# A hybrid decoder trunk on one core: which output block is kept in a gate's tile, where short rows of logits stand, and how the last square of a norm is added

## The chip, the cores and the metric

The kernel runs on one core of a Trainium2 chip. Its time is the device time of one execution in microseconds (us). The core's engines run their own instruction streams and wait for each other through semaphores: TensorE (PE) multiplies matrices into PSUM, VectorE (DVE) and ScalarE (ACT) work on tiles, GpSimd (POOL) and SyncE (SP) here mostly issue transfers (DMA). An engine takes its instructions strictly in order, so an instruction that waits holds all that stand behind it.

## The reference

Two layers over 1024 positions of width 1024, each with a residual and an RMS norm ahead, and a last norm behind. All is float32.

```python
def reference(x, norm_g, final_g, lru_..., fox_...):
    for i in range(DEPTH):                       # DEPTH = 2
        h = rms_norm(x, norm_g[i])
        if i % N_MIXERS == 0:
            x = x + lru_mixer(h, ...)
        else:
            x = x + fox_mixer(h, ...)
    return rms_norm(x, final_g)

def rms_norm(x, g):
    y = x * rsqrt(mean(x * x, axis=-1) + EPS)
    return y * g

# lru_mixer: u = h @ w_in; a causal convolution of 4 taps; two gates, block-diagonal (12 blocks of 128);
#            a linear recurrence along the positions; times silu(gate); @ w_out
# fox_mixer: 16 heads of 64; logits = q @ k.T / 8 + (cum_q - cum_k), causal; softmax; @ v; times silu(gate); @ w_out
```

## The kernel before

**Form of the data.** Activations lie transposed: 128 channels of a block on the partitions, the positions along the free axis, in two halves of 512 (`HALF`; c or h is 0 or 1). A float32 product is made of three matmuls: each operand is split into a high part and a remainder (`to_hi`, `to_lo`: hh and hl, wh and wl, yhh and yhl), and hh·wh, hh·wl and hl·wh are summed in PSUM. A product of a 128x512 block with k input blocks is thus 3k matmuls of 128x512.

**Order.** A scheduler places the instructions of each engine by a timeline of its own; the code gives priorities, and `issue_after` ties an instruction behind another. So a small edit can move instructions elsewhere.

**Layer 0** (to about 432 us). `square_x` squares the eight input blocks of a half on ScalarE and adds seven of them into one tile on VectorE; the eighth square stays in its own tile. `norm_row` sums both tiles over the channels with two products with a matrix of ones (`rsrow`), accumulated, then a square root (ScalarE) and a reciprocal (VectorE) give the row `rs` by which products are scaled. Then twelve channel blocks run through input product (`ups`, `gps`), convolution (`us`, `xc`, its split `xch`, `xcl`), gates (`gate`), recurrence and output. `softplus` computes small constants of all blocks from one 128x12 parameter (`sp_e`, `sp_d`, `sp_q`), on VectorE.

**Boundary** (about 432 to 475 us). The last output product is added to the residual, which is written to memory as `x1d`, split and squared again (`squares`). Here too the last square of a half is left in its own tile (`wait=db == KT - 1`), and `inv_rms` sums over channels with matmuls of one column per 128 positions (`sscol`), as many as there are tiles.

**Layer 1** (about 475 to 1057 us): sixteen heads. For a head hd and a half c, `maxima` makes four rows of logits (`S`; row i has 128(i+1) columns: rows 0 to 3 for c = 0, rows 4 to 7 for c = 1), VectorE masks them and takes the maximum, ScalarE the exponential (`p`), the two split it into half-precision parts (`pp`), and SyncE issues a DMA that transposes them (`pT`). `weigh` multiplies pT with the values into `O`. `run(order, ...)` (L855) lays these out on TensorE: in `ORDER` and `LAST`, "1" is a row of logits, "0" a step of weighing and "." a step of fill, which is six matmuls of some other product. A head has two runs: the first weighs its half 0 and makes its rows 4 to 7, the second weighs its half 1 and makes rows 0 to 3 of the next head. `ORDER` holds for heads 0 to 11, `LAST` for the rest. Fill is the projections of the next heads (`gps`, `vps` among the value heads 3, 7 and 11, where new values are made), and from head 12 on the blocks (db, c) of the output projection, in the order (0,0), (1,0), (0,1), (1,1), (2,0), (2,1), (3,0), (3,1), (4,0) and so on to (7,1).

**Output blocks.** `partial` makes them, over the first six pairs of heads, 18 matmuls in a bank of PSUM (`ops1`, printed `ops`, two banks in turn). Its residual comes from `x1d` by a DMA of POOL into a tile, VectorE adds the product (L924), and a DMA of POOL writes the sum back to `x1d`, 256 KB each way. Tiles come from a ring of two (`rpool`, tag "R", name `xp`). Blocks that `kept` names are not written back: their tile lives until the end. Block 3 is kept in a tile of the tag "sg" (name `x3`, two halves, one for block 3 and one for block 2), in which pair 6's gate lay; that tile is free when `gated(13, 1)` (L839) has read it. Blocks 5, 6 and 7 lie in a tile of four, `x4` (`T0`), which is free when an earlier head's keys are done, and which also has room for block 4. In the end `residual` fetches the blocks that were written back, by SyncE's queue, and `turned` makes the output.

**Queues.** SyncE issues, in one queue, loads of weights, the transpositions, and the fetches of `residual`. POOL issues the loads and stores of `partial`.

Of the kernel before, what the change touches and what calls it, by code (L numbers as in the profile page):

```python
# [22 lines left out]
KT = 8  # L23
# [2 lines left out]
HD = 64  # L26
EPS = 1e-6
GROUP = 2
ORDER = "1.1..1.1..00", "1.1.1.1...0000"
LAST = "1..1..1..1..0.0", "1..1.1..1..0..0.0.0"  # L30
NEG = -1e30
PSUM = bass.MemoryType.PSUM
# [8 lines left out]
def trunk(ctx: ExitStack, tc: tile.TileContext, xt, w0, wg, wo0, pc, gn, gf, w1, wv, wf, bf, wo1, out):  # L41
# [14 lines left out]
    def fetch(to, src):  # L56
        loads_by[0].dma_start(to, src)
# [70 lines left out]
    def gemm_steps(ps, pairs, chunks=(slice(0, HALF),)):  # L128

        pairs = list(pairs)  # L130
        for cs in chunks:
            o = ps[:, cs]
            for i, ((wh, wl), (xh, xl)) in enumerate(pairs):
                matmul(o, wh, xh[:, cs], start=i == 0, stop=False)
                matmul(o, wl, xh[:, cs], start=False, stop=False)
                matmul(o, wh, xl[:, cs], start=False, stop=i == len(pairs) - 1)
                if i % 2:
                    yield
# [29 lines left out]
    def squares(parts, x, tile, eng=nc.vector, wait=False):  # L168

        sq = tile()  # L170
        nc.scalar.activation(sq, x, AF.Square)
        if not parts or wait:
            parts.append(sq)
        else:
            eng.tensor_tensor(parts[0], parts[0], sq, ALU.add)
# [12 lines left out]
    with ExitStack() as l0:  # L188
# [9 lines left out]
        def pair():  # L198
            return tuple(hpool.tile([P, HALF], F32R, tag=t, name=t) for t in ("hh", "hl"))
# [35 lines left out]
        k = 0  # L235
# [12 lines left out]
        sums = [[], []]  # L248

        def split_x(h, layer=0):  # L250
            for k, (hi, lo) in enumerate((raw, hT)[layer][h]):
                g_ = gnt[:, layer, k : k + 1]
                x = xs[h][k]
                to_hi(hi, x, nc.scalar, scale=g_)
                nc.vector.scalar_tensor_tensor(lo, x, g_, f32(hi), ALU.mult, ALU.subtract)
                yield
# [4 lines left out]
        def square_x(h):  # L261
            to = acc[:, halves[h]]
            sums[h].append(to)
            for k in range(KT):
                z = sq[k % 4] if k else to
                nc.scalar.activation(z, xs[h][k], AF.Square)
                if k == KT - 1:
                    sums[h].append(z)
                elif k:
                    nc.vector.tensor_tensor(to, to, z, ALU.add)  # L270
                yield

        def rms_row(parts, rs, *rms):
            return inv_rms(parts, ps.tile([P, HALF], F32, tag="O", name="sscol")[:, : HALF // P], rs, *rms)
# [199 lines left out]
        def mm3(o, w, x, start, stop):  # L474
            (wh, wl), (xh, xl) = w, x
            matmul(o, wh, xh, start=start, stop=False)
            matmul(o, wl, xh, start=False, stop=False)
            matmul(o, wh, xl, start=False, stop=stop)
# [5 lines left out]
        def value_bounds():  # L484

            for _ in range(2):
                nc.vector.tensor_tensor(vsq, vsq, gnt[:, 1].unsqueeze(1).to_broadcast([P, 4, KT]), ALU.mult)
            all_ = ps.tile([P, 4 * KT], F32, tag="O", name="vnorm")
            matmul(all_, onesf, vsq.rearrange("p a b -> p (a b)"), start=True, stop=True)
            nc.vector.tensor_reduce(  # L490
                scale_v, all_.rearrange("p (a b) -> p a b", b=KT), mybir.AxisListType.X, ALU.add
            )
            nc.scalar.activation(scale_v, scale_v, AF.Sqrt, bias=tiny, scale=SEQ / TOP / TOP)
            nc.vector.tensor_scalar(unit_v, scale_v, 0.5 / TOP, None, ALU.mult)
            nc.vector.reciprocal(scale_v, scale_v)

        wl = [w for d0 in range(0, KT, 2) for w in out_weights(NB // 2 - 1, d0)]
        for h, cs in enumerate(halves):
            y = [tuple(z[:, cs] for z in p) for p in ys[-2:]]
            hT[h] = [pair() for k in range(KT)]  # L500
            parts = split_x(h, 1)
            sums = []
            for d0 in range(0, KT, 4):
                pts = []
                for db in range(d0, d0 + 4):
                    if db % 2 == 0:
                        two = ps.tile([P, 2, HALF], F32, tag="S", name="ops")
                    pts.append(two[:, db % 2])
                    mm3(pts[-1], wl[db][0], y[0], True, False)
                for db, o in enumerate(pts, d0):  # L510
                    mm3(o, wl[db][1], y[1], False, True)
                    x = xs[h][db]
                    nc.vector.tensor_tensor(x, x, o, ALU.add)  # L513
                    nc.sync.dma_start(x1d[h, :, db], x)
                    next(parts)
                    squares(
                        sums,
                        x,
                        lambda: nrm.tile([P, HALF], F32, tag="sq" if db else "ss", name="sq", bufs=2),
                        wait=db == KT - 1,  # L520
                    )
            rms_row(sums, rs1[h], rms1[h])
            if h == 0:
                value_bounds()
            nc.vector.tensor_tensor(
                rv[:, :, 4 * h : 4 * h + 4],
                rms1[h].unsqueeze(1).to_broadcast([P, 4, 4]),
                scale_v.unsqueeze(2).to_broadcast([P, 4, 4]),
                ALU.mult,
            )  # L530
# [7 lines left out]
    with ExitStack() as l1:  # L538
# [207 lines left out]
        def g_units(pair, hs=(0, 1)):  # L746

            if hs[0] == 0:
                sgs[pair] = at.tile([P, SEQ], F32, tag="sg", name="sg1")
                gw[0] = list(weights(w1[16 + pair], lo_eng=low(pair)))  # L750
            sg = sgs[pair]

            def use(h, pt):
                g_ = sg[:, h * HALF : (h + 1) * HALF]
                nc.scalar.activation(g_, pt, AF.Tanh, scale=0.5)
                nc.vector.scalar_tensor_tensor(g_, g_, 1.0, pt, ALU.add, ALU.mult)

            yield from project(gw[0], use, hs)
# [88 lines left out]
        def chain(*gens):  # L847
            for g in gens:
                yield from g
# [42 lines left out]
        def split_out(db):  # L892
            if db < KT and db not in wo:
                wo[db] = list(weights(wo1[db, :, :6], lo_eng=nc.vector))
# [5 lines left out]
        homes = {}  # L900

        def home(db):

            if db == 3:
                two = at.tile([P, 2, HALF], F32, tag="sg", name="x3")
                homes[3], homes[2] = two[:, 0], two[:, 1]
            elif db == 5:
                four = tu.tile([P, 4, HALF], F32, tag="T0", name="x4")
                homes.update((4 + i, four[:, i]) for i in range(4))
            return homes[db]  # L910

        def partial(todo):

            for db, c in todo:
                split_out(db)
                if c if db < 2 else not c:
                    split_out(db + 1)

                kept = c == 0 and db in (3, 5, 6, 7)
                x = home(db) if kept else rpool.tile([P, HALF], F32, tag="R", name="xp")  # L920
                nc.gpsimd.dma_start(x, x1d[c, :, db])
                pt = ps.tile([P, HALF], F32, tag="g", name="ops1")
                yield from gemm_steps(pt, zip(wo[db], [y1[c][pair] for pair in range(6)]))
                nc.vector.tensor_tensor(x, x, pt, ALU.add)  # L924
                if not kept:
                    nc.gpsimd.dma_start(x1d[c, :, db], x)
# [5 lines left out]
        def residual(c, q):  # L932

            cs = slice(q * 256, (q + 1) * 256)
            if c == q == 0:
                two = tu.tile([P, 2, HALF], F32, tag="U0", name="x0")
                homes[0], homes[1] = two[:, 0], two[:, 1]
                for d in (0, 1, 2, 4):
                    fetch(homes[d], x1d[c, :, d])
            if c == 0:  # L940
                return [homes[d][:, cs] for d in range(KT)]
            xs = [wpool.tile([P, 2, 256], F32, tag=("wl", "wh")[q], name="x1") for d in range(4)]
            for d, x in enumerate(xs):
                fetch(x, x1d[c, :, 2 * d : 2 * d + 2, cs])
            return [x[:, i] for x in xs for i in range(2)]
# [107 lines left out]
        for hd in range(HEADS):  # L1053
# [22 lines left out]
            elif pair < 6:  # L1076
                fill = chain(g_units(pair + 1), kq_units(pair + 2, ((1, (0,)),)))
            first, second = LAST if hd > 11 else ORDER
            if hd == HEADS - 1:
# [35 lines left out]
        for q in range(2):  # L1115
            left[1, q] = residual(1, q)
# [70 lines left out]
```

## Time and profile before

| | |
|---|---|
| median of three runs | 1079.46 us (1077.64 to 1081.99) |
| the profiled execution's own time | 1079.6 us |
| its span | 1077.8 us |
| mean granted clock of TensorE | 0.995 |
| bytes moved | 142.55 MB |

The profile is that of one execution. A busy share says how long an engine had work in it, not whether it was at its peak. Waits are put down to the semaphore that came last; where the engine named had long been done, another event was it, often a DMA. Matmuls overlap: the duration of one (0.39 us) is longer than the step from one start to the next (0.23 us), and the step is what a matmul costs.

### The profile page before, as it was taken

The numbers are of one execution on the slowest core, as the hardware profiler recorded it, in microseconds if no ns is written. First come the engines' busy times: TensorE is split into PE (matmuls) and PEld (weight loads), VectorE is DVE, ScalarE is ACT, GpSimd is POOL, SyncE is SP. The second block draws the span as 40 slices with busy tenths as digits, with TensorE's granted clock in tenths as the row PEclk, the third lists the DMA queues.
The fourth block names the chain that finished last, engine by engine and source line by source line (L and its number), as shares of the span: only waits on it lengthen the run. The fifth ranks groups of instructions, "written<-read, shape, count | busy, mean of one in ns | idle before, by whom it ended". The sixth has DMA issues, their size and how long they took to land. (4 is left out here: it accounts for less than half of the span.)

```text
span 1077.8 us, 14962 instructions
## 1 busy us (share of the span) xinstructions
PE 1048.0 (97%) x5100; PEld 843.7 (78%) x5100; DVE 782.1 (73%) x1444; ACT 621.6 (58%) x1082; POOL 113.2 (11%) x91
## 2 busy tenths in 40 slices
PE   9999999999999999999999999999999999997997
PEld 7788888888888887797777797767977779765776
DVE  7889657766776589947878848788488866774665
ACT  8488453655465564745757636566466655653454
POOL 1322021202220210030000000000000000011200
PEclk9999999999999999999999999999999999998999
DMA  7111211222122112535878957899578885988994
GB/s 251 60 43 50 64 59 54 64 69 64 54 70 68 49 54 69 158 94 134 157 174 192 176 135 155 179 190 191 139 153 188 174 191 131 226 210 225 224 193 157
DMA packets 218508, 142.55 MB, mean 132 GB/s; under 512 B 161792, under 2 KB 178688, under 8 KB 218432
## 3 DMA queue, kind: packets, MB, share of 16 engines
q1 hardware_dynamic: 216032, 133.74, 52.3%
q0 software_dynamic: 2400, 7.87, 2.4%
q8 instruction: 40, 0.66, 0.3%
q14 instruction: 36, 0.29, 0.1%
HBM read 63.82 MB, written 14.81 MB: 73 GB/s over the span
## 5 line engine op out<-in xcount | busy, mean ns | idle before, releaser
L60 PE MATMUL gps<-hh,wh 128*128 128x512 f32 x576 | 227.3, 395 | 0.0
L60 PE MATMUL gps<-hh,wl 128*128 128x512 f32 x576 | 226.4, 393 | 0.8 <-DVE wl L101 0.7
L60 PE MATMUL gps<-hl,wh 128*128 128x512 f32 x576 | 226.6, 393 | 0.0
L90 ACT CAST wh<-wf 128x512 fp32r<-128x512 f32 (+2 forms) x162 | 97.3, 605 | 113.5 <-PE ops L60 43.0
L791 ACT ACTIVATE p<-S,m 128x128 f32<-128x128 f32 (+7 forms) x128 | 94.7, 740 | 67.6 <-DVE m L786 37.9
L101 POOL TENSOR_TENSOR wl<-wf,wh 128x512 fp32r<-128x512 f32 (+1 forms) x50 | 91.9, 1850 | 369.9 <-ACT wh L90 358.3
L60 PEld LDWEIGHTS gps<-hl,wh 128*128 128x128 f32 x576 | 108.4, 188 | 25.0 <-issue 0.5
L60 PEld LDWEIGHTS gps<-hh,wl 128*128 128x128 f32 x576 | 108.6, 189 | 22.5 <-DVE wl L101 1.0
L60 PEld LDWEIGHTS gps<-hh,wh 128*128 128x128 f32 x576 | 108.5, 188 | 21.6
L800 DVE SCALAR_TENSOR_TENSOR pp<-p,sums,pp 128x128 f16<-128x128 f32 (+7 forms) x128 | 103.1, 814 | 19.1 <-ACT pp L92 17.9
L92 ACT ACTIVATE pp<-p,sums 128x128 f16<-128x128 f32 (+7 forms) x128 | 95.5, 770 | 31.2 <-DVE sums L798 15.6
L786 DVE CUSTOM_DVE_ANT_0 S<-S,mask 128x128 f32<-128x128 f32 (+7 forms) x128 | 97.2, 760 | 16.9 <-PE S L60 15.6
L60 PE MATMUL S<-T,U 96*128 96x512 f32 (+7 forms) x384 | 94.3, 355 | 8.1 <-ACT p L791 8.0
L101 DVE TENSOR_TENSOR wl<-wf,wh 128x512 fp32r<-128x512 f32 x112 | 74.4, 668 | 25.8 <-ACT wh L90 25.6
L60 PEld LDWEIGHTS S<-T,U 128*128 128x128 f32 (+1 forms) x384 | 67.9, 190 | 26.2 <-ACT p L791 14.3
L389 DVE TENSOR_TENSOR x<-x,ops 128x512 f32<-128x512 f32 x80 | 54.1, 683 | 41.5 <-PE ops L60 41.4
L60 PE MATMUL ups<-hh,wh 128*128 128x512 f32 x192 | 75.6, 395 | 1.2 <-ACT hh L92 1.2
L60 PE MATMUL ups<-hl,wh 128*128 128x512 f32 x192 | 76.6, 399 | 0.2
L60 PE MATMUL ops<-yh,wl 128*128 128x512 f32 x192 | 75.7, 394 | 0.9 <-DVE wl L101 0.9
L60 PE MATMUL ops<-yh,wh 128*128 128x512 f32 x192 | 75.8, 396 | 0.5 <-DVE x L513 0.5
L60 PE MATMUL ups<-hh,wl 128*128 128x512 f32 x192 | 75.8, 395 | 0.0
L60 PE MATMUL O<-pT,v 128*128 128x512 f16 (+3 forms) x396 | 71.3, 322 | 3.8 <-DMA pT<-pp 3.6
(188 smaller groups left out, 1985.8 us busy)
## 6 DMA issues: line engine op xcount, KB each, us to landing
wf<-in_w SPq DMA_DIRECT2D x106, 256.0 KB
wf<-in_wo SPq DMA_DIRECT2D x64, 128.0 KB
T<-qkh SPq DMA_DIRECT2D x64, 128.0 KB
U<-qkh SPq DMA_DIRECT2D x64, 128.0 KB
x<-in_xt SPq DMA_DIRECT2D x16, 256.0 KB
wvf<-in_wv SPq DMA_DIRECT2D x32, 128.0 KB
x1d<-x SPq DMA_DIRECT2D x16, 256.0 KB
wf<-in_wv SPq DMA_DIRECT2D x16, 256.0 KB
```

Source lines behind the costliest of these rows:

```text
L60: pe[0] = nc.tensor.matmul(*args, **kw)
L90: nc.scalar.copy(hi, src)
L92: nc.scalar.activation(hi, src, AF.Copy, scale=scale)
L101: return eng.tensor_tensor(lo, src, f32(hi), ALU.subtract)
L389: nc.vector.tensor_tensor(x, x, pt, ALU.add)
L786: nc.vector.tensor_tensor_reduce(S[:, :n], S[:, :n], mask[:, SEQ - n :], -1.0, -NEG, ALU.add, ALU.min, accum_out=m)
L791: seen[0] = nc.scalar.activation(p, S[:, :n], AF.Exp, bias=m, scale=-1.0, accum_out=sums[:, i : i + 1])
L800: nc.vector.scalar_tensor_tensor(both[:, :, 1], p, r, both[:, :, 0], ALU.mult, ALU.subtract)
```

## The change

Three parts. The block kept in the gate's tile is 4 instead of 3; the tile's other half then belongs to 3 and the tile of four holds 2, 5, 6 and 7. (3,0) goes through the ring and is written back; `residual` fetches 0 to 3. In the second run of heads 0 to 11, S(2) stands one step of fill later and S(3) two. In the norm of layer 0, and in the second half of that at the boundary, VectorE adds the last square too, so that one tile is summed over the channels.

```diff
-ORDER = "1.1..1.1..00", "1.1.1.1...0000"
+ORDER = "1.1..1.1..00", "1.1..1..1.0000"
...
             for k in range(KT):
                 z = sq[k % 4] if k else to
                 nc.scalar.activation(z, xs[h][k], AF.Square)
-                if k == KT - 1:
-                    sums[h].append(z)
-                elif k:
+                if k:
                     nc.vector.tensor_tensor(to, to, z, ALU.add)
...
-                        wait=db == KT - 1,
+                        wait=h == 0 and db == KT - 1,
...
         def home(db):
-            if db == 3:
+            if db == 4:
                 two = at.tile([P, 2, HALF], F32, tag="sg", name="x3")
-                homes[3], homes[2] = two[:, 0], two[:, 1]
+                homes[4], homes[3] = two[:, 0], two[:, 1]
             elif db == 5:
                 four = tu.tile([P, 4, HALF], F32, tag="T0", name="x4")
-                homes.update((4 + i, four[:, i]) for i in range(4))
+                homes.update(zip((2, 5, 6, 7), (four[:, i] for i in range(4))))
             return homes[db]
...
-                kept = c == 0 and db in (3, 5, 6, 7)
+                kept = c == 0 and db > 3
...
-                for d in (0, 1, 2, 4):
+                for d in range(4):
                     fetch(homes[d], x1d[c, :, d])
```

**POOL's queue around head 14.** `x1d_94` is the residual in memory; `x3` and `x4` are the gate's tile and the tile of four; in the piece of before xp_9119 is block (2,1), xp_9220 is (3,1), xp_9289 is (4,0), xp_9327 is (4,1), and x3_9163 is (3,0). Before:

```order
L921 DMA xp_9220<-x1d_94 128x512
L926 DMA x1d_94<-xp_9119 128x512
L921 DMA xp_9289<-x1d_94 128x512
L921 DMA x3_9163<-x1d_94 128x512
L926 DMA x1d_94<-xp_9220 128x512
L921 DMA xp_9327<-x1d_94 128x512
L921 DMA x4_9400<-x1d_94 128x512 x3
```

Now, with xp_9116 for (2,1), xp_9160 for (3,0), xp_9218 for (3,1), x3_9287 for (4,0), xp_9324 for (4,1) and xp_9462 for (5,1):

```order
L919 DMA xp_9218<-x1d_94 128x512
L924 DMA x1d_94<-xp_9160 128x512
L919 DMA x3_9287<-x1d_94 128x512
L919 DMA xp_9324<-x1d_94 128x512
L924 DMA x1d_94<-xp_9218 128x512
L919 DMA xp_9462<-x1d_94 128x512
L919 DMA x4_9397<-x1d_94 128x512 x3
```

The load into the gate's tile stands one block later, behind a store of (3,0) that was not there.

**SyncE's queue in the same place.** Rows 4 to 7 of head 14 are the transpositions of 10, 12, 14 and 16 blocks. The gate's tile receives its other half from memory here. Before:

```order
L57 DMA x3_9163<-x1d_94 128x512
L802 DMA_TRANSPOSE pT_9193<-pp_9203 128x10x128
L57 DMA wf_9388<-in_wo1 128x512
L57 DMA wf_9394<-in_wo1 128x256
L802 DMA_TRANSPOSE pT_9193<-pp_9240 128x12x128
L57 DMA x0_9697<-x1d_94 128x512 x2
L802 DMA_TRANSPOSE pT_9193<-pp_9269 128x14x128
L802 DMA_TRANSPOSE pT_9193<-pp_9313 128x16x128
```

Now:

```order
L57 DMA x3_9287<-x1d_94 128x512
L800 DMA_TRANSPOSE pT_9190<-pp_9200 128x10x128
L57 DMA wf_9385<-in_wo1 128x512
L800 DMA_TRANSPOSE pT_9190<-pp_9238 128x12x128
L57 DMA wf_9391<-in_wo1 128x256
L57 DMA x0_9694<-x1d_94 128x512 x2
L57 DMA x4_9397<-x1d_94 128x512
L800 DMA_TRANSPOSE pT_9190<-pp_9267 128x14x128
L800 DMA_TRANSPOSE pT_9190<-pp_9311 128x16x128
```

The first fetch now brings block (3,0), which was written back shortly before; it was (2,0). A fetch into the tile of four is new ahead of the last two transpositions.

**TensorE in a value head.** The end of the second run of head 3: `gps` is a projection, `vps` the values' projection. Before, the last rows ahead of the weighing product are

```order
L60 MATMUL gps_5387<-hh,wl 128x512
L60 MATMUL gps_5387<-hl,wh 128x512
L60 LDWEIGHTS v_3840
L60 MATMUL O<-pT,v_3840 128x512
L60 LDWEIGHTS v_3840
```

and now, from the last row of logits on,

```order
L60 MATMUL S<-T_3673,U 128x512 x2
L60 MATMUL gps_5371<-hh,wh 128x512
L60 MATMUL gps_5371<-hh,wl 128x512
L60 MATMUL gps_5371<-hl,wh 128x512
L60 MATMUL gps_5371<-hh,wh 128x512
L60 MATMUL gps_5371<-hh,wl 128x512
L60 MATMUL gps_5371<-hl,wh 128x512
L60 MATMUL vps<-wh,hh 128x256
L60 MATMUL vps<-wh,hl 128x256
L60 MATMUL vps<-wl,hh 128x256
```

with eleven more rows of `vps` behind, and then the weighing product. Six instead of eighteen matmuls of `gps` stand between the last row of logits and the weighing, and fourteen of `vps` that used to follow it.

**VectorE in the first norm.** `m` and `ti` hold squares, `rs` is the norm's row, `us` opens the convolution. Before:

```order
L270 TENSOR_TENSOR m_203<-m_203,ti 128x512
L283 RECIPROCAL rs<-rs 128x512
L216 TENSOR_SCALAR sp_d<-sp_e 128x12
L228 TENSOR_SCALAR hba<-pct 128x12
L229 TENSOR_SCALAR hbx<-pct 128x12
L283 RECIPROCAL rs<-rs 128x512
L217 RECIPROCAL sp_d<-sp_d 128x12
L297 TENSOR_TENSOR us<-ups,rs 128x1024
```

Now, from the middle of the softplus on:

```order
L222 SCALAR_TENSOR_TENSOR sp_q<-sp_q,sp_d 128x12 x8
L223 SCALAR_TENSOR_TENSOR sp_q<-sp_q,sp_e 128x12
L224 TENSOR_SCALAR sp_d<-pct 128x12
L225 SCALAR_TENSOR_TENSOR sp_d<-sp_q,sp_d 128x12
L226 TENSOR_SCALAR c_105<-sp_d 128x12
L227 TENSOR_SCALAR nc_106<-sp_d 128x12
L281 RECIPROCAL rs<-rs 128x512
L295 TENSOR_TENSOR us<-ups,rs 128x1024
```

The whole softplus now stands ahead of the second reciprocal; before, all but three of its rows stood behind it, among the convolution's.

## Prediction

> **What bounds the kernel now.** I read the page first, for whether one engine carries the span; then the list of waits of TensorE, for what it lacks; then the timeline around the longest wait, and the chain of waits for its cause.
>
> ```profile
> span 1077.8 us, 14962 instructions
> PE 1048.0 (97%) x5100; PEld 843.7 (78%) x5100; DVE 782.1 (73%) x1444; ACT 621.6 (58%) x1082; POOL 113.2 (11%) x91
> PEclk9999999999999999999999999999999999998999
> ...
> PE S L60 <- ACT p L791: 8.0, 9, 2.1
> PE ops L60 <- DVE sums L797: 5.5, 1, 5.5
> PE O L60 <- DMA pT<-pp: 3.6, 5, 1.4
> ```
>
> TensorE works 1048.0 of 1077.8 us, so a change can gain in two ways only: fewer or faster matmuls, or less of the 29.8 us in which TensorE is idle. The waits (engine, line and what it waited for: us in total, times, longest) put 17.1 of those us in three rows: logits that wait for ScalarE's exponential to free a slot, one wait of 5.5 us of an output block, and weighing products that wait for the transposed weights. The clock row has one dip, an 8 near the end. The timeline shows that dip and the 5.5 us to be one event (start, duration, and in brackets the idle time before):
>
> ```profile
> 984.27 1.08 PE L60 MATMUL S<-T,U 128*128 128x512 f32 x4 [0.31 <-ACT p L791]
> 990.87 0.80 PE L60 MATMUL ops<-yhh,wh 128*128 128x512 f32 x1 [5.52 <-DVE sums L797]
> 991.47 0.63 PE L60 MATMUL ops<-yhh,wl 128*128 128x512 f32 x1
> 991.89 0.63 PE L60 MATMUL ops<-yhl,wh 128*128 128x512 f32 x1
> ...
> 996.16 1.13 PE L60 MATMUL S<-T,U 128*128 128x512 f32 x4
> ...
> 997.36 0.40 PE L60 MATMUL ops<-yhh,wl 128*128 128x512 f32 x1
> 997.59 0.40 PE L60 MATMUL ops<-yhl,wh 128*128 128x512 f32 x1
> ...
> core 0: us, PE busy (x) PEld busy (x) DVE busy (x) ACT busy (x) POOL busy (x), PEclk, DMA share, GB/s
> 990.80:996.20 5.40, 5.33 (x13) 4.17 (x14) 3.93 (x11) 3.08 (x4) 0.99 (x2) 0.50 0.48 143
> ```
>
> After the gap the matmuls follow each other 0.42 us apart instead of 0.23, at a granted clock of 0.50, from 990.87 to 996.16: twelve of them, so 12 x (0.425 - 0.232) = 2.3 us. The event costs 5.5 + 2.3 = 7.8 us. Its cause:
>
> ```profile
> 984.40 0.69 DVE L839 TENSOR_TENSOR yo<-yo,sg 128x512 f32<-128x512 f32 x1
> ...
> 985.38 0.54 POOL L921 DMA_DIRECT2D x<-x1d  x1 [3.53 <-DVE sums L798]
> ...
> 985.38 4.72 DMA x<-x1d
> ...
> 990.13 0.69 DVE L924 TENSOR_TENSOR x<-x,ops 128x512 f32<-128x512 f32 x1 [2.93 <-DMA x<-x1d]
> ```
>
> Block (3,0) is kept in the tile of pair 6's gate. Its residual can be fetched only when the last reader of the gate (L839, done at 985.09) is through; POOL issues it at 985.38, it takes 4.72 us, VectorE adds at 990.13, and only the add frees the bank of PSUM that the next block's matmuls need. The row of waits names "sums L797", the small instruction beside the add; the add is what counts. All twelve slow matmuls and the gap follow from one load that starts too late.
>
> **Part A, the kept block.** The gate's tile now serves (4,0), two blocks later in the order of work ((3,0), (3,1), (4,0)). A block is 18 matmuls, 18 x 0.23 = 4.2 us, so its residual is wanted more than 8 us later than before; 4.72 + 0.69 us after the gate is released it is there. (3,0) goes through the ring of two small tiles instead, and its fetch needs no gate. So the 7.8 us go; what is late next?
>
> ```profile
> 981.32 0.54 POOL L921 DMA_DIRECT2D xp<-x1d  x1 [4.13 <-DMA x1d<-xp]
> ...
> 985.42 0.37 SPq L57 DMA_DIRECT2D x<-x1d  x1
> 987.26 2.27 SPq L802 DMA_TRANSPOSE pT<-pp  x1
> ...
> 1003.73 10.69 DMA pT<-pp
> ...
> 1014.47 1.04 PE L60 MATMUL O<-pT,v 128*128 128x512 f16 x4 [0.80 <-DMA pT<-pp]
> ```
>
> The next product that needs something from outside is the weighing of head 14's second half at 1014.47, which already waits 0.80 us for the transposition of row 7, landed at 1003.73 + 10.69 = 1014.42. Without the event TensorE is there 7.8 us sooner, at 1014.47 - 0.80 - 7.8 = 1005.9. Row 7's logits (996.16) would stand at 988.4; from logits to the start of the transposition it took 1003.73 - 996.16 = 7.6 us, and VectorE loses the 2.93 us pause in which it worked for nothing, so I add those: start about 998.9. The transposition took 10.69 us beside three residual loads and a store; without such company it would be perhaps half, so it lands between 1004 and 1009.6, middle 1007. The product resumes then at about 1007.8, allowing 0.8 us as now, and gains 1014.47 - 1007.8 = 6.7. Two of the moved blocks' adds come close to the matmuls that want their bank; I take two small stalls like the 0.31 of the first timeline row off. **A = 6.0 us**, bounds 0 (the transposition lands when it does now; the event only moves) and 8.6 (7.8 and the 0.8 too).
>
> [...]
>
> **Part B, the spread logits.** In twelve of the heads the second run now has two more steps of fill between S(1) and S(3), and the same six in all. Which waits could that take?
>
> ```profile
> 620.52 2.97 PE L60 MATMUL O<-pT,v 128*128 128x512 f16 x16 [1.38 <-DMA pT<-pp]
> ...
> 623.62 0.28 PE L60 MATMUL vps<-wl,hh 128*128 128x256 f32 x1
> 623.74 0.28 PE L60 MATMUL vps<-wh,hh 128*128 128x256 f32 x1
> ...
> 715.28 0.62 PE L60 MATMUL S<-T,U 128*128 128x384 f32 x2 [1.62 <-ACT p L791]
> ...
> 841.85 0.62 PE L60 MATMUL S<-T,U 128*128 128x384 f32 x2 [1.07 <-ACT p L791]
> 848.82 2.99 PE L60 MATMUL O<-pT,v 128*128 128x512 f16 x16 [0.29 <-DMA pT<-pp]
> ...
> 867.01 3.32 DMA wf<-in_w
> ...
> 871.54 0.74 PE L60 MATMUL S<-T,U 128*128 128x512 f32 x2 [2.11 <-ACT p L791]
> ```
>
> Each S wait above sits in such a run, and one step later (6 x 0.23 = 1.4 us) or two (2.8 us) covers it. But in an ordinary head the weighing product comes after the same fill and needs the row-7 transposition, which no edit makes earlier: at 848.82 it waits 0.29 us although S had just lost 1.07. There the gain turns into a wait of O. It is kept in the three heads whose fill holds value products: there the order now puts fourteen of them ahead of the first weighing product, 14 x 0.12 = 1.7 us (step from 623.62 to 623.74), enough for the 1.38 at 620.52. The 2.11 at 871.54 is in the last of these heads; it comes from a weight cast on ScalarE that waits for a load (landed 870.33), and two steps cover it. **B = 1.4 + 2.0, less 0.1 = 3.3 us**; bounds 0 (all turns into waits of O) and 1.38 + 1.62 + 1.07 + 2.11 = 6.2.
>
> **Part C, the squares.** Each norm's last square is now added by VectorE, so the sum over rows needs one product instead of two in each half of the first norm, and eight fewer column records in the second half of the second norm.
>
> ```profile
> 19.02 1.02 PE L60 MATMUL rsrow<-m,onesf 128*128 128x512 f32 x2
> ...
> 20.11 0.40 PE L60 MATMUL gps<-hl,wh 128*128 128x512 f32 x1
> ...
> 440.37 1.84 PE L60 MATMUL sscol<-onesf,sq 128*128 128x1 f32 x16
> 442.07 0.47 PE L60 MATMUL ops<-yh,wh 128*128 128x512 f32 x1
> ```
>
> From 19.02 to 20.11 TensorE did one product of the norm (a pair of records) and one ordinary matmul: 1.09 - 0.23 = 0.86 us; two of them go, 1.72. The sixteen column records took 442.07 - 440.37 = 1.70; half is 0.85. The adds cost VectorE 0.69 each (the shape of the 990.13 row), in stages where it isn't what TensorE waits for. **C = 2.6 us**, bounds 0 (the adds delay the norm by as much) and 2.6.
>
> But C also turns an order round in the first norm: VectorE now runs seventeen more small instructions of the softplus before the second reciprocal.
>
> ```profile
> 36.26 3.35 DVE L283 RECIPROCAL rs<-rs 128x512 f32<-128x512 f32 x1
> ...
> 48.50 0.16 DVE L222 SCALAR_TENSOR_TENSOR sp_q<-sp_q,sp_d 128x12 f32<-128x12 f32 x1
> ...
> 50.05 1.23 DVE L101 TENSOR_TENSOR xcl<-xc,xch 128x1024 fp32r<-128x1024 f32 x1
> ...
> 55.35 0.62 PE L60 MATMUL gate<-xcl,wgh 128*128 128x512 f32 x2
> ```
>
> The reciprocal may end 17 x 0.16 + 0.69 (the add) = 3.4 us later; the lower half of the convolution is ready at 51.28 and wanted at 55.35, a cover of 4.1 us. I cost that at nothing; those small instructions no longer stand among the convolution's, and the order also puts the first gates a dozen matmuls later.
>
> **Sum.** 6.0 + 3.3 + 2.6 = 11.9, and 1079.6 (the profiled execution) - 11.9 = **1067.7 us**. That execution stands 0.1 us from the median of the runs, 1079.46, so nothing is corrected.
>
> **Rivals.**
> First, the transpositions bound the late stage. For it: 1014.47 already waits for one, and three loads, a store and two transpositions share the engines in that stretch. Against it: row 7's logits come 7.8 us sooner. Then A is 0 and the time 1079.6 - 3.3 - 2.6 = 1073.7. [...]
>
> Second, slower: SyncE's queue is held. Its fetch of block 3's first half (now from the copy in memory) must wait for the store of (3,0), and stands ahead of the transpositions of rows 4 to 7. That store is issued about 985.0 and takes 4.1 us (the wait at 981.32 is such a store), so the fetch moves from 985.42 to 989.6 and the 987.26 transposition to about 990: 2.7 later. One more block is fetched on this queue ahead of rows 6 and 7: 256 KB at 143 GB/s, 1.8 us. Row 7 would land at 1014.42 + 4.5 = 1018.9, TensorE wait 13 us for it and be slow after (2.3): A = -(4.5 + 2.3) = -6.8, and where B gives nothing, 1079.6 + 6.8 - 2.6 = 1083.8 (1080.5 with B). It decides from a landing 0.3 us later than now without B, 3.6 with it. Against it: the wait begins only if the fetch reaches the head of the queue before the store has landed, and the transpositions' inputs are themselves earlier now.
>
> Third, the spread pays nothing, since O's wait takes it up in the value heads too: 1079.6 - 6.0 - 2.6 = 1071.0.
>
> Fourth, the late reciprocal is not covered, since VectorE is TensorE's busiest helper (73% on the page), and its 3.4 us appear: 1067.7 + 3.4 = 1071.1.
>
> **How the numbers follow.** Forecast 0.58, with its own range 1062.2 (A and B at their upper bounds, 1079.6 - 8.6 - 6.2 - 2.6) to 1073 (B at nothing and A at 4); first rival 0.14, second 0.12, third and fourth 0.08 each. Range: 1062 to 1080, from those upper bounds to the second rival with B (1080.5), cut a little. Half a per cent, 5.4 us, is about what a measurement of this kernel can tell from no change. Faster than 1074.1: the forecast nearly whole (0.56), half of the first rival (0.07), and 0.07 from each of the last two, 0.77. Slower than 1084.9: half of the second rival, 0.06. Between them 0.17.
>
> **What would show it.** A: the wait of 5.5 us on "sums" is gone, the clock row has no dip near 990, and the wait before head 14's second weighing is under 4 us; over 8 there means the first or second rival, and row 4's transposition after 989.5 means the second. B: TensorE's waits on "p L791" fall from 8.0 to under 4, and those on pT don't grow by as much; 620.52's wait vanishes. C: two records each of rsrow and eight of sscol fewer; the first gates without a wait, else the fourth rival. I am wrong if a new wait over 4 us stands between 985 and 1020, or if TensorE idles between 20 and 60 us.

## The result, and the profile after

| | before | changed |
|---|---|---|
| median of six runs | 1079.46 us | 1096.56 us |
| lowest to highest | 1077.64 to 1081.99 | 1092.08 to 1100.08 |
| ratio, with its 95% interval | | 1.0156 (1.0127 to 1.0185) |
| profiled execution, its span | 1079.6, 1077.8 us | 1094.07, 1092.3 us |
| mean granted clock of TensorE | 0.995 | 0.986 |

The change costs 17.1 us by the medians, 14.5 us between the two profiled executions. The page of the changed kernel, in the lines that answer to those of before (busy time, the clock in forty slices), and behind it the largest rows of what TensorE waited for (us in total, times, longest us):

```profile
span 1092.3 us, 14947 instructions
PE 1052.4 (96%) x5088; PEld 849.5 (78%) x5088; DVE 787.7 (72%) x1447; ACT 622.8 (57%) x1082; POOL 108.2 (10%) x91
PEclk9999999999999999999999999999899999999899
...
PE vps L60 <- ACT wh L90: 12.9, 3, 5.0
PE O L60 <- DMA pT<-pp: 9.6, 5, 4.4
PE gate L60 <- ACT th L320: 1.6, 1, 1.6
PE S L60 <- ACT p L789: 1.4, 2, 0.7
```

Two of the rows are as predicted: the wait of 5.5 us on "sums" is gone, and the waits of the logits fell from 8.0 to 1.4 us. But 12.9 us stand in a row that before did not have at all: the values' projection waits, three times, for the cast of its weights. The waits on the transposed attention weights (pT) grew from 3.6 to 9.6.

Where the time went is read from the first logits of row 4 (shape 128x320), which every head makes at the same place in its order. For head 3 and head 4, first of before and then of the changed kernel (timeline: start, duration):

```profile
596.32 0.84 PE L60 MATMUL S<-T,U 128*128 128x320 f32 x4
...
646.10 0.76 PE L60 MATMUL S<-T,U 128*128 128x320 f32 x4
```

```profile
599.04 0.86 PE L60 MATMUL S<-T,U 128*128 128x320 f32 x4
...
652.73 0.77 PE L60 MATMUL S<-T,U 128*128 128x320 f32 x4
```

Head 3, a value head, took 49.78 us before and 53.69 now: 3.91 us more. The same subtraction along the program, with the first column sum of the boundary as the mark for layer 0:

| stage, up to the start of | before | changed | lost in the stage |
|---|---|---|---|
| layer 0, boundary's first column sum | 440.37 | 443.63 | +3.3 |
| boundary and heads 0 to 2, row 4 of head 3 | 596.32 | 599.04 | -0.5 |
| value head 3, row 4 of head 4 | 646.10 | 652.73 | +3.9 |
| heads 4 to 6, row 4 of head 7 | 724.64 | 729.34 | -1.9 |
| value head 7, row 4 of head 8 | 772.95 | 784.14 | +6.5 |
| heads 8 to 10, row 4 of head 11 | 851.62 | 861.91 | -0.9 |
| value head 11, row 4 of head 12 | 901.86 | 918.40 | +6.3 |
| heads 12 to 14, row 4 of head 15 | 1022.89 | 1037.36 | -2.1 |

The three value heads lose 16.7 us, layer 0 another 3.3; all the rest gains 5.4. The sum is the 14.5 us between the spans.

**The value heads.** Timelines of SyncE's queue, ScalarE and TensorE of the changed kernel in head 3:

```profile
629.75 1.31 SPq L800 DMA_TRANSPOSE pT<-pp  x1
...
631.74 0.42 SPq L57 DMA_DIRECT2D wf<-in_wv  x1
...
635.87 0.62 ACT L90 CAST wh<-wf 128x512 fp32r<-128x512 f32 x1 [7.40 <-DMA wf<-in_wv]
...
636.54 0.58 PE L60 MATMUL vps<-wh,hh 128*128 128x256 f32 x1 [3.65 <-ACT wh L90]
636.92 0.41 PE L60 MATMUL vps<-wh,hl 128*128 128x256 f32 x1
...
core 0: us, PE busy (x) PEld busy (x) DVE busy (x) ACT busy (x) POOL busy (x), PEclk, DMA share, GB/s
637.00:639.40 2.40, 2.40 (x13) 2.40 (x13) 0.21 (x1) 0.00 (x0) 0.00 (x0) 0.50 0.92 200
```

A group's value weights come in four loads, all on SyncE's queue. Here the fourth is issued at 631.74, behind a transposition; the cast has it at 635.87, and TensorE, which had come to the products that need it, waits 3.65 us and then works at half clock (0.50). In the trace of before the third and the fourth load went out together, 13.9 us after the head's row 4 instead of 32.7:

```profile
610.21 0.92 SPq L57 DMA_DIRECT2D wf<-in_wv  x2
```

The schedule's rows of SyncE's queue say what moved. Of the changed kernel, with rows between left out:

```
292 L57 DMA wf_5450<-in_wv 128x512
293 L800 DMA_TRANSPOSE pT_5164<-pp_5244 128x14x128
294 L800 DMA_TRANSPOSE pT_5164<-pp_5265 128x16x128
...
307 L800 DMA_TRANSPOSE pT_5313<-pp_5414 128x8x128
308 L57 DMA y1d_3665<-yo_5141 128x512
309 L57 DMA wf_5456<-in_wv 128x512
```

In the schedule of before the two loads stand at 290 and 291, next to each other. Now six transpositions and ten other rows stand between them (the expectations below say eight; it is six). SyncE's records in the trace come in the order of these rows: the third load at 614.08, the six transpositions from 614.62 to 631.06, the fourth load at 631.74. A transposition takes as its input the softmax of a row of logits; between 612 and 633 us the queue's waits put 4.3 us, the longest of 3.4, down to the last piece of such a softmax (L800 <- DVE pp). So the load is held by work with which it has nothing to do. The fourteen products of values that the new order puts ahead of the weighing don't wait: they run from 621.30 to 622.97 without a pause. The wait at 636.54 is that of a later product of the same projection, the first that needs the fourth load.

**The late stage.** Head 14's second weighing, and in the chain of waits what came ahead of it:

```profile
1026.27 1.89 PE L60 MATMUL O<-pT,v 128*128 128x512 f16 x4 [4.36 <-DMA pT<-pp]
...
1011.47 8.32 DMA x<-x1d
1019.79 6.43 DMA pT<-pp
```

The block's wait has gone. The same weighing product, which before waited 0.80 us for row 7's transposition (1014.47), now waits 4.36 us.

### The profile page after: what moved, and what is told of

Its sections match the earlier page's. It is cut to its first block, busy times and chain, and to the rows that moved or that the text cites. A ratio compares the mean times of both kernels' runs of the same rounds, so it can differ in the third digit from the quotient of the medians.

```text
span 1092.3 us, 14947 instructions
## 1 busy us (share of the span) xinstructions
PE 1052.4 (96%) x5088; PEld 849.5 (78%) x5088; DVE 787.7 (72%) x1447; ACT 622.8 (57%) x1082; POOL 108.2 (10%) x91
## 5 line engine op out<-in xcount | busy, mean ns | idle before, releaser
L101 POOL TENSOR_TENSOR wl<-wf,wh 128x512 fp32r<-128x512 f32 (+1 forms) x50 | 86.8, 1750 | 378.3 <-ACT wh L90 378.2
L60 PE MATMUL vps<-wh,hh 128*128 128x256 f32 (+1 forms) x256 | 76.0, 298 | 13.8 <-ACT wh L90 12.9
```

The source lines that it names most:

```text
L60: pe[0] = nc.tensor.matmul(*args, **kw)
L101: return eng.tensor_tensor(lo, src, f32(hi), ALU.subtract)
```

## Experiments

"Before" was run beside each group on the same chip; its medians were 1079.6 to 1081.3 us.

**Each part alone.** `a_kept` has only the kept block moved (the edits in `home`, `kept` and `residual`), `b_spread` only

```diff
-ORDER = "1.1..1.1..00", "1.1.1.1...0000"
+ORDER = "1.1..1.1..00", "1.1..1..1.0000"
```

and `c_square` only the two edits of the squares.

> Only the kept block is moved (block 4 in the gate's tile). If the changed kernel's late stage is as its trace shows (head 14's second weighing waits 4.4 us for row 7's transposition, then nine matmuls at half clock), this part gains about 2 us: near 1077.5, and the wait stands in the late stage again. If the prediction's 6.0 us are right and the loss there came from the other parts, 1073.5. A wait on value weights (ACT wh) in the middle of the kernel is expected by neither.

> Only the order of the second run is changed. The theory of the held load (the fourth load of a group's value weights now stands behind eight transpositions in SyncE's queue) expects three waits of vps on ACT wh of 3.6 to 5 us, in all some 16.5 us lost in the value heads with the slow clock behind them, less about 2 gained in the other heads: near 1094. The rival, that the waits come from the parts together, expects a time within 3 us of before and the loads where they were. The prediction expected 1076.

> Only the last square is added by VectorE, in both norms. If the late second reciprocal is what makes layer 0 longer, the first boundary sum (sscol) starts about 3 us later than before, and the time is near 1081.6 (3.3 lost ahead of it, 1.1 gained at the boundary). If layer 0's loss came from elsewhere (the scheduler's other moves), it shows none of it and 1077. The prediction expected 1077.

| | median | ratio to before, 95% interval |
|---|---|---|
| a_kept | 1077.20 | 0.9969 (0.9949 to 0.9989) |
| b_spread | 1097.89 | 1.0150 (1.0112 to 1.0188) |
| c_square | 1084.94 | 1.0031 (1.0008 to 1.0054) |

The parts add up to the whole (0.9969 x 1.0150 x 1.0031 = 1.0150). The spread logits alone make it slow: TensorE's waits in `b_spread` are those of the whole change.

```profile
PE vps L60 <- ACT wh L90: 11.5, 3, 4.5
PE O L60 <- DMA pT<-pp: 8.3, 6, 2.7
PE ops L60 <- DVE sums L797: 5.9, 1, 5.9
```

The third row is the block's wait of before, since the block is not moved here.

**The load's place in the queue.** `full_pool_loads` is the whole change, with the value weights loaded by POOL's queue, which has nothing else to do in that stage (its one record between 600 and 640 us is the load shown below):

```diff
+                if not ex:
+                    loads_by[0] = nc.gpsimd
                 parts += split_weights(src, (2, 256 + ex), nc.scalar, nc.gpsimd if ex else nc.vector)
+                loads_by[0] = nc.sync
```

> The whole change, but the value weights of the three later groups are loaded by POOL's queue instead of SyncE's; the fourteen or so vps matmuls still stand ahead of the weighing product. If the load's place in SyncE's queue is the cause, the waits of vps on ACT wh go and the time falls by about 16 us, to near 1080. If the loads are slow because the DMA engines are full, or if it is the vps ahead of the weighing that cost, the waits stay and the time stays above 1090.

It took 1077.93 us, 0.9970 (0.9946 to 0.9993): 18.6 us less than the whole change. The products of values still stand ahead of the weighing (sixteen now), and they wait for nothing; the row of 12.9 us is gone from the list. In head 3 POOL issues the fourth load at 611.34, as soon as its buffer is free, 13.3 us after the head's row 4, where SyncE's queue had it 32.7 us after:

```profile
611.34 0.54 POOL L57 DMA_DIRECT2D wf<-in_wv  x1 [14.60 <-DVE wl L101]
...
PE O L60 <- DMA pT<-pp: 9.9, 7, 4.2
PE S L60 <- ACT p L792: 2.4, 3, 1.4
PE gps L60 <- ACT wh L90: 1.9, 3, 0.7
```

From its issue to its landing the load took 5.2 us here, and in the changed kernel 4.1 from its issue to the cast (631.74 to 635.87). So the bytes were not too slow to come, and the products were not in the wrong place: the load was issued too late.

**Which head moves it.** The new order was given to single heads; the schedule then shows the late fourth load whenever the head ahead of a value head (head 2, 6 or 10) has it, and the products of values ahead of the weighing only when the value head has it too. `b_third_only` has it in heads 2, 6 and 10 alone, `b_not_third` in all others of the twelve:

```diff
             first, second = LAST if hd > 11 else ORDER
+            if hd < 12 and hd % 4 == 2:
+                second = "1.1..1..1.0000"
```

> The new order of the second run in three of every four heads, also in the heads that make new values, but not in the head ahead of each of these; the four loads of value weights stand where they were in SyncE's queue, and no vps stand ahead of the weighing. The theory of the held load expects no wait of vps on ACT wh above 1 us and a time at or a little below before: 1078 to 1081. If the new order in a value head itself is what costs, 12 us or more are lost.

> The new order only in the one head ahead of each value head; the value heads have the old one, and no vps stand ahead of the weighing, but the fourth load of value weights stands sixteen rows later, behind eight transpositions. The theory of the held load expects three waits of vps on ACT wh of 2 to 5 us all the same, and 1088 to 1096. If the vps moved ahead of the weighing are the cause, there are none and the time is within 2 us of before.

`b_third_only` took 1100.65 us, 1.0155 (1.0113 to 1.0198), more than expected; `b_not_third` 1077.39 us, 0.9967 (0.9947 to 0.9987). Of `b_third_only`:

```profile
PE vps L60 <- ACT wh L90: 12.5, 3, 4.7
PE O L60 <- DMA pT<-pp: 9.6, 6, 2.8
```

By the marks of the table above, the three value heads of `b_third_only`, with a late load and no moved product, lose 16.6 us (53.97, 55.35 and 55.65 us against 49.78, 48.31 and 50.24), as much as in the whole change; the rest of its loss lies in other heads and was not followed. Nine heads with the new order and no late load gain 3 us. That settles the cause in the value heads. Why the scheduler puts the load there when an earlier head's logits move was not tried.

**The late stage.** Three fetches of SyncE and three loads of POOL, 256 KB each, are issued close to row 7's transposition, in the changed kernel from 1010.68 and from 1011.47 on. `a_fetch_late` is `a_kept` with the first tied behind row 3 of head 15, `a_loads_late` is `a_kept` with two of the second tied behind stores:

```diff
+                with tc.issue_after(turns[-5].ins):
+                    for d in range(4):
+                        fetch(homes[d], x1d[c, :, d])
```

```diff
+                if kept and db > 5:
+                    with tc.issue_after(stores[-1].ins):
+                        nc.gpsimd.dma_start(x, x1d[c, :, db])
```

> The kept block is moved as in a_kept, and SyncE's four fetches of residuals (256 KB each) stand behind row 3 of head 15, so none stands ahead of head 14's transpositions. If the second rival's place (SyncE's queue with its fetches) holds row 7's transposition, the 5.2 us wait of head 14's second weighing falls under 2 and the time comes to about 1073. If it is the DMA engines' load or POOL's three loads, the wait stays above 3.5 us and the time near 1077.

> The kept block is moved as in a_kept, and POOL's loads for (6,0) and (7,0) are issued behind the stores of (5,1) and (6,1), instead of three loads at once beside row 7's transposition. If POOL's loads are what the transposition shares the engines with, the wait of head 14's second weighing falls under 3 us (two of the seven transfers beside it are gone) and the time to about 1075. If SyncE's queue holds it, the wait stays near 5 and the time near 1077.

`a_fetch_late` took 1076.12 us, 0.9951 (0.9925 to 0.9977), `a_loads_late` 1075.27 us, 0.9933 (0.9908 to 0.9958). Head 14's second weighing in `a_kept` (with the transposition from its chain of waits), `a_fetch_late` and `a_loads_late`. The rows of VectorE make the last piece of row 7's softmax, and the last row of SyncE's queue in each starts row 7's transposition:

```profile
996.27 1.28 DVE L800 SCALAR_TENSOR_TENSOR pp<-p,sums,pp 128x1024 f16<-128x1024 f32 x1 [0.68 <-ACT pp L92]
996.40 4.38 SPq L802 DMA_TRANSPOSE pT<-pp  x1
1000.87 7.17 SPq L802 DMA_TRANSPOSE pT<-pp  x1
1010.47 1.89 PE L60 MATMUL O<-pT,v 128*128 128x512 f16 x4 [5.23 <-DMA pT<-pp]
...
1000.87 9.56 DMA pT<-pp
```

```profile
999.30 1.28 DVE L800 SCALAR_TENSOR_TENSOR pp<-p,sums,pp 128x1024 f16<-128x1024 f32 x1 [0.68 <-ACT pp L92]
1000.61 5.42 SPq L802 DMA_TRANSPOSE pT<-pp  x1
1008.83 1.02 PE L60 MATMUL O<-pT,v 128*128 128x512 f16 x4 [0.58 <-DMA pT<-pp]
...
1011.81 0.76 PE L60 MATMUL ops<-yhh,wh 128*128 128x512 f32 x1 [1.96 <-DVE x L924]
```

```profile
994.94 1.29 DVE L800 SCALAR_TENSOR_TENSOR pp<-p,sums,pp 128x1024 f16<-128x1024 f32 x1 [0.68 <-ACT pp L92]
999.80 3.48 SPq L802 DMA_TRANSPOSE pT<-pp  x1
1004.76 1.04 PE L60 MATMUL O<-pT,v 128*128 128x512 f16 x4 [0.88 <-DMA pT<-pp]
```

Taking away either set of transfers removes the wait, but in two different ways:

| | row 7's softmax done | its transposition starts | held by | from the start to the weighing |
|---|---|---|---|---|
| before | 1003.70 | 1003.73 | 0.0 | 10.7 |
| changed kernel | 1014.23 | 1019.79 | 5.6 | 6.5 |
| a_kept | 997.55 | 1000.87 | 3.3 | 9.6 |
| a_fetch_late | 1000.58 | 1000.61 | 0.0 | 8.2 |
| a_loads_late | 996.23 | 999.80 | 3.6 | 5.0 |

In `a_kept` the transposition starts 3.3 us late: SyncE's queue has the three fetches ahead of row 6's transposition, which starts at 996.40 though its input was done at 994.14, and row 7's stands behind that one, whose record ends at 1000.78. Without the fetches in the queue nothing is held (0.0 us), but from its start to the weighing it is still 8.2 us instead of 9.6. With two of POOL's loads away it is as late (3.6 us), but from its start to the weighing it is 5.0 us. So both the queue and the transfers beside it made the wait of 5.23 us, and less of either is enough (0.58 and 0.88 us). In the changed kernel row 7's is held longest, since row 6's, with the same transfers beside it, takes 7.5 us there (1012.23 to 1019.70). In `a_fetch_late` the next product waits instead, for a block's add. Between row 4 of head 14 and row 4 of head 15 `a_loads_late` is 7.6 us shorter than before (1013.57 - 975.21 against 1022.89 - 976.89), where `a_kept` is 1.1 shorter; the end gives 2.4 of it back.

**The first norm.** `c_softplus_after` ties the softplus behind the second reciprocal, since the prediction had named it; `c_adds_first` ties the first root and reciprocal behind the last square and the last add instead; `c_adds_first_sp` does both.

```diff
-                norm_row(1)
+                done = norm_row(1)
                 with tc.issue_after(done.ins):
                     softplus()
```

```diff
-                done = norm_row(0)
+                with tc.issue_after(tail[0].ins), tc.issue_after(tail[1].ins):
+                    done = norm_row(0)
```

> As c_square, but the softplus is tied behind the second reciprocal of the first norm instead of the first. If the seventeen small instructions ahead of that reciprocal are what made layer 0 longer, the second reciprocal starts near 37 us instead of 41, TensorE's waits at 45 and 105 us go, and the time comes to about 1078, 2 to 3 us under before. If VectorE's adds themselves (or other moves of the schedule) are the cause, the waits stay and the time is 1082 or more.

> As c_square, but the first norm's root and reciprocal are tied behind the last square and the last add of the second half; the softplus stays where the schedule puts it, ahead of the second reciprocal in part. If the reciprocal ahead of the adds is the cause, the second reciprocal starts within 2 us of before's 36.3, no wait of more than 0.5 us stands at 100 to 106 us, and the time is 1077 to 1079 (before near 1080). If the adds themselves cost it, the waits stay and the time is near 1083 again.

> As c_adds_first, with the softplus behind the second reciprocal as well. If the order on VectorE is the whole matter, the second reciprocal starts at or before 36.3, and the squares bring what was counted for them: 1.7 + 0.9 = 2.6 us, 1077.5 with before at 1080. If the softplus costs nothing where it is, the same time as c_adds_first.

| | median | ratio to before, 95% interval | boundary's first column sum, against before |
|---|---|---|---|
| c_square | 1084.94 | 1.0031 (1.0008 to 1.0054) | +3.4 |
| c_softplus_after | 1082.47 | 1.0028 (1.0008 to 1.0048) | +1.6 |
| c_adds_first | 1080.07 | 0.9991 (0.9973 to 1.0009) | -1.8 |
| c_adds_first_sp | 1082.51 | 1.0008 (0.9989 to 1.0026) | +2.3 |

The last column is of one profiled execution each; in ten executions with the first norm as before, this mark lies between 440.07 and 441.10. VectorE in `c_square`:

```profile
28.88 3.35 DVE L281 RECIPROCAL rs<-rs 128x512 f32<-128x512 f32 x1 [0.62 <-ACT rs L280]
...
36.62 0.68 DVE L268 TENSOR_TENSOR m<-m,ti 128x512 f32<-128x512 f32 x1
...
41.27 3.35 DVE L281 RECIPROCAL rs<-rs 128x512 f32<-128x512 f32 x1 [1.26 <-ACT rs L280]
```

and in `c_adds_first`:

```profile
28.64 1.49 DVE L270 TENSOR_TENSOR m<-m,ti 128x512 f32<-128x512 f32 x2
30.04 3.35 DVE L285 RECIPROCAL rs<-rs 128x512 f32<-128x512 f32 x1
...
36.97 3.35 DVE L285 RECIPROCAL rs<-rs 128x512 f32<-128x512 f32 x1
```

The schedule of the changed kernel puts the first reciprocal, 3.35 us, ahead of the last adds, which the other half's row sum needs; so the second reciprocal starts at 41.27 in `c_square` (39.65 in the changed kernel) instead of 36.26. With the adds ahead of it, it starts at 36.97, TensorE's waits at 46 and 105 us are gone, and layer 0 is as much shorter as was counted for the two products less. Moving the softplus alone hardly mends the start: 39.33, where 37 was expected and three executions with the softplus ahead have 39.65, 40.34 (`full_pool_loads`) and 41.27; still, layer 0 is 1.8 us shorter than in `c_square`. With both ties it is 36.91, but two new waits of 1.1 and 0.9 us, for weights, stand at 101 and 103 us; what moved there was not followed. Nor does the gain of `c_adds_first` last: it is 2.6 us ahead of before at row 4 of head 1 (542.30 against 544.91) and 0.4 at row 4 of head 15 (1022.50 against 1022.89). Why was not tried.

**Together.** `all_mended` takes the whole change with POOL's loads of value weights, the spread loads of (6,0) and (7,0), and the softplus behind; `ab_mended` leaves the first norm as it was before; `ab_mended_nt` is `ab_mended` with SyncE's loads and the new order in nine heads; `all_mended2` and `all_mended3` are `ab_mended` with the first norm of `c_adds_first_sp` and `c_adds_first`.

> The whole change with each cause taken away: value weights loaded by POOL's queue, POOL's loads for (6,0) and (7,0) behind the stores of (5,1) and (6,1), the softplus behind the second reciprocal. If the three causes add up, 1080.5 less 5.3 (kept block with spread loads), less 3.4 (spread logits with the load's place mended) and less 2.5 (squares): near 1069.5, between 1067 and 1073. If the gains hide each other, 1074 to 1077.

> As all_mended, but the first norm keeps its two tiles of squares, and the softplus its place; the boundary's second norm has the one tile. By the same sum 1080.5 - 5.3 - 3.4 - 0.9 = 1071; against all_mended it shows whether the first norm's change pays once it is mended (1.7 us by the profile).

> As ab_mended, but the value weights stay on SyncE's queue, and the new order is left out in the head ahead of each value head (as in b_not_third). By the sum 1080.5 - 5.3 - 3.2 - 0.9 = 1071, the same as ab_mended if the queue is the whole matter; above 1074 if POOL's queue brought more than the mend.

> ab_mended (1070.3) with the first norm's change in the order of c_adds_first_sp: 1.7 us under ab_mended, near 1068.5, if the order is the cause; 1.5 us above it, as all_mended, if it isn't.

> ab_mended with the first norm's change in the order of c_adds_first. If the 1.75 us of layer 0 reach the end, 1.5 to 2 us under ab_mended_again, near 1068.5; if the attention stage gives them back, as in c_adds_first, the same time within 1 us.

> The kernel of ab_mended once more, as the neighbour of all_mended3: 1070 to 1071, 0.9908 of before within its interval.

| | median | ratio to before, 95% interval |
|---|---|---|
| all_mended | 1071.77 | 0.9931 (0.9907 to 0.9955) |
| ab_mended | 1070.26 | 0.9908 (0.9881 to 0.9936) |
| ab_mended_nt | 1071.90 | 0.9924 (0.9894 to 0.9953) |
| all_mended2 | 1072.60 | 0.9927 (0.9902 to 0.9951) |
| all_mended3 | 1072.09 | 0.9924 (0.9903 to 0.9945) |
| ab_mended_again | 1071.14 | 0.9911 (0.9888 to 0.9935) |

The versions with each cause taken away are 8 to 9 us faster than before. `ab_mended`, run twice, has the lowest ratios with 0.9908 and 0.9911, but its intervals overlap those of the others, so no order among them is shown. `ab_mended_nt`, which avoids the late load by the order of the logits and leaves SyncE's queue its loads, gains as much within the intervals; so nothing beyond the load's place is shown for POOL's queue. The first norm's change shows no gain even in its best order: `all_mended3` has layer 0 shorter by 1.6 us in its profile, and its time is not under that of its neighbour.

## Why the prediction was wrong

**The frame held.** TensorE bounds the kernel (busy 1048.0 of 1077.8 us before, 1052.4 of 1092.3 changed), its waits and its clock set the time, and the event at 985 us came from the late load into the gate's tile: that wait was gone in every run with the kept block moved.

**Part B failed, in one step:** its lower bound, "bounds 0 (all turns into waits of O)". It priced the waits on TensorE that the new order could take or turn into others; that the order could make something else late was put at nothing, without a reason. The step with the fourteen products held: they follow each other at 0.12 us, the wait at 620.52 did go, and they wait for nothing themselves. But the new order in the head ahead of each value head moved the fourth load of value weights sixteen rows down SyncE's queue, behind six transpositions, and the products that need it came to wait. Both schedules showed it; the prediction and the part on the change show SyncE's queue only around head 14, where a trouble was expected. The waits cost 12.9 us and the clock behind them (0.50 in a stretch of 2.0 to 2.4 us behind each) some more, and the three heads lost 16.7 where 3.3 were to be gained. No rival had this place. For the other heads nothing was counted, since the wait was to pass on to the transposition: there the logits' waits went, those on the transposition took most of it over, and 2 to 3 us stayed.

**Part A was right in kind and too large.** 6.0 was forecast; heads 12 to 14 gained 2.1, and the part alone brought 3.2 (1080.35 us to 1077.20). The mis-sized term is the landing of row 7's transposition, "between 1004 and 1009.6, middle 1007", and both of its pieces were too small. Its start, "about 998.9", was 1000.87 in `a_kept`, since it was held in SyncE's queue for 3.3 us; its length, "perhaps half" of 10.69, was 9.56 with six transfers of 256 KB beside it. It landed at 1010.43, 5.2 us after TensorE was ready. The first rival, which held 0.14, had the length. The second, with 0.12, had the queue: its fetch "ahead of rows 6 and 7" did hold them, though the step that it priced highest, row 4's transposition 2.7 us later, came to 1.1 (input done at 987.32, start at 988.42). With the loads spread, the stage is 7.6 us shorter, near the 7.8 of the event; by the medians the part then brings 5.3 (1080.57 to 1075.27).

**Part C had its gains right and its cover wrong.** At the boundary the changed kernel gained 1.15 us where 0.85 was counted (443.63 to 547.02 against 440.37 to 544.91, up to row 4 of head 1), and layer 0 with the adds first gained 1.75 where 1.72 was counted. But "the reciprocal may end 17 x 0.16 + 0.69 = 3.4 us later", with a cover of 4.1, costed at nothing, failed twice. Its 3.4 is met by luck: in the changed kernel the reciprocal started 3.4 us later (39.65 against 36.26), in `c_square` 5.0, because the first reciprocal had been put ahead of the adds, and not for the softplus. The rows of VectorE in the part on the change begin behind that place; the schedule has it. And the cover was read at the first gates, but TensorE sooner needed the bank of `ups`, which VectorE frees when it makes `us` behind the reciprocal:

```profile
44.48 0.48 PE L60 MATMUL ups<-hh,wh 128*128 128x512 f32 x1 [0.95 <-DVE us L295]
...
101.46 0.50 PE L60 MATMUL ups<-hh,wh 128*128 128x512 f32 x1 [0.45 <-ACT wh L90]
103.98 0.80 PE L60 MATMUL gate<-xch,wgh 128*128 128x512 f32 x1 [1.57 <-ACT th L320]
```

The first of these waits, between 20 and 60 us, is one that the prediction had named as a sign of being wrong. The fourth rival had the symptom and a wrong reason for it.

**What the range missed.** 1062 to 1080 rested on the parts that the prediction had priced. The loss lay in an instruction that the change doesn't name, on a queue that the prediction showed in one place only.

## What to carry to other kernels

Where a scheduler rewrites the queues, compare every queue over its whole length, and above all look for what moved behind something that waits or is long: here a load behind six transpositions was issued 32.7 us after its head's row 4 instead of 13.9, and adds behind a reciprocal of 3.35 us went with a second reciprocal at 41.27 instead of 36.97 us (`c_square` and `c_adds_first`). Where the order of products changes, follow the inputs of those that come behind back to their loads, too, and not only those that were moved. And when a long stall goes, list the transfers that it had kept apart; spreading them was worth about as much here (0.9933 of before with both, `a_loads_late`) as the edit that removed the stall (0.9969 alone, `a_kept`).

## What was not expected of the hardware

A granted clock of 0.50 stood here behind shorter pauses than the 5.52 us of before: behind 3.65 us in head 3 (above), and once behind still less. In the changed kernel the waits of 0.45 and 1.57 us at 101 to 104 us, shown above, were followed by matmuls at a granted clock of 0.50; in `c_square` the same two waits (0.42 and 1.56, for the same instructions) were followed by 1.00. The stretches behind them, first of the changed kernel and then of `c_square` (the third number from the end is the clock):

```profile
104.50:107.00 2.50, 2.50 (x7) 1.94 (x6) 2.50 (x2) 2.47 (x4) 0.48 (x1) 0.50 0.39 113
```

```profile
106.00:108.50 2.50, 2.50 (x13) 2.04 (x12) 2.50 (x3) 2.47 (x4) 0.57 (x1) 1.00 0.43 134
```

The seven matmul steps behind the second wait took 3.13 us and 1.73, so the same pause cost 1.4 us more in one execution than in the other. What decides was not tried.
